# Splitting a second matrix ahead of a pair's first products, and a later gate after a pair, in a two-layer decoder trunk

## The chip, the cores and the metric

The kernel runs on one core of a Trainium2 chip. The metric is the device time of one execution in microseconds (us); the time of a kernel is the median of several runs. Lower is better.

## What is computed

Two decoder layers over 256 positions of width 1024, fp32 throughout. The even layer has sparse attentions and a dense SwiGLU; the odd layer has a dilated attention and an expert SwiGLU: every token goes to two of eight experts, each with three matrices, 1024 x 3584, 1024 x 3584 and 3584 x 1024.

```python
def swiglu(x, w1, w3, w2):
    return (jax.nn.silu(x @ w1) * (x @ w3)) @ w2
...
def moe_swiglu(x2d, router, w1, w3, w2):
    logits = (x2d @ router).astype(F32)
    top_val, top_exp = lax.top_k(logits, TOP_K)
    gates = jax.nn.softmax(top_val, axis=-1)
...
        return (jax.nn.silu(xb @ w1[e]) * (xb @ w3[e])) @ w2[e]
```

The change is about the expert SwiGLU. Every matrix of it is read once from memory.

## The kernel before

**Two ways to multiply.** TensorE (PE) is fast with operands of type fp32r, which keep less of a number than fp32. So a tile of a matrix is *split*: `split` (L226) calls `parts` (L221), where ScalarE (ACT) writes `hi`, the tile rounded to fp32r (L222), and VectorE (DVE) writes `lo`, the tile minus `hi` (L223). `mm3` (L231 to L234) then makes three fp32r products: `hi` with the activations' high part, `lo` with it (L233), `hi` with their low part (L234); the first of them is L232. The `hi` and `lo` tiles, 128 x 1024 each, come from a pool of five buffers (`WB`). The other way, `up2` (L285) and the first half of `down` (L651), multiplies the raw fp32 tile without a split, with the tokens of *two* experts side by side: each has 64 columns of PE and its own half of the output's partitions.

**Blocks.** Experts 0 to 3 hold up to 128 tokens and are worked on alone; experts 4 and 5, and 6 and 7, hold up to 64 each and are worked on as pairs. Each expert's 3584 columns are cut into seven chunks of 512 (the last pair's seventh into two of 256). One chunk of an expert, or of a pair, is a *block*. `swiglu` goes through a list `items` in which two alone blocks and one pair block follow each other; there are 28 alone blocks and 15 pair blocks, here counted from 0, and the last two are pairs. Block N below is the N-th pair block.

**What a block does**, in the order of the program (`swiglu`, the loop over `items`): the first matrix's products start (`up` or `up2`, a generator that is advanced by `step(u, 2)`); then `gate_T` transposes the gated activations of the *preceding* block (L625 if that is a pair, L632 if alone) and splits them into `gh` on ACT and `gl` on DVE (L634, L635); then the rest of the first products, and the silu on ACT into `sl` (L700); then `down` for the preceding block: it loads the second matrix, splits it and adds its products to the accumulators `acc`; then the third matrix's products, and the multiply of `sl` by them on DVE (L713), which the next block's gate transposes. For the first chunk of an expert (`pre`) the preceding block's `down` is worked off before the first products.

For an alone block, `down` reads and splits so:

```python
                for q in range(r, nr if last else r + 2, m):
                    v = load(w2, c0 // P + q, m, 0, D)
                    ws += [split(v[:, j:j + 1, :]) for j in range(m)]
```

A load (L218) is a DMA of 1 MB, issued on SyncE (SP) into a ring of slots named `raw`. Each engine works in order. The order in which the program is written is not the final one: a scheduler places each instruction by when its operands are ready, and keeps the program's order as the tie's. What stands on each engine in the end is a list that can be printed; the rows below come from it.

Of the kernel before, what the change touches and what calls it, by code (L numbers as in the profile page):

```python
# [17 lines left out]
P = 128  # L18
D = 1024
# [133 lines left out]
def trunk(ctx: ExitStack, tc: tile.TileContext, a, out, R=6, WB=5, NF=16):  # L153
# [17 lines left out]
    def nm(s):  # L171
        uid[0] += 1
        return f"{s}_{uid[0]}"
# [31 lines left out]
    def raw():  # L205
        slot = "raw"
        if late:
            slot = late.pop(0)
            if slot == "x":
                return xp.tile([P, 2 * D], F32, tag="x", name=nm("raw"), bufs=2)  # L210
            late.append(slot)
        return rawp.tile([P, 2048], F32, tag=slot, name=nm("raw"), bufs=R if slot == "raw" else 1)

    def load(w, r0, nr, c0, ncol):
        t = raw()
        v = t[:, :nr * ncol].rearrange("p (k f) -> p k f", k=nr)
        src = w.at(r0, nr, c0, ncol)
        nc.sync.dma_start(v if len(src.shape) == 3 else t[:, :nr * ncol], src)  # L218
        return v

    def parts(v, hi, lo, by):  # L221
        A.activation(hi, v, AF.Copy)  # L222
        by.tensor_sub(lo, v, hi.bitcast(F32))  # L223
        return hi, lo

    def split(v, by=V):  # L226
        _, k, n = v.shape
        t = [wp.tile([P, 1024], F32R, tag=q, name=nm(q)) for q in ("hi", "lo")]
        return parts(v, *(q[:, :k * n].rearrange("p (k f) -> p k f", k=k) for q in t), by)
# [34 lines left out]
    def up(outs, w, c0, ncol, sta, ws=None, between=None):  # L264


        if ws is None:
            for q in pieces(w, c0, ncol, 2):
                for o, s in zip(outs, sta):
                    products(o, s, *q)  # L270
                yield
        else:
            for i in range(len(sta)):
                for q in ws:
                    products(outs[i], sta[i], *q)
                if i == 0 and between:
                    between()

    def up2(o, ws, c0, ncol, sta):

        for r in (0, 4):
            vs = [load(w, r, 4, c0, ncol) for w in ws]
            for k in range(4):
                for i, v in enumerate(vs):
                    TE.matmul(o[i * 64:(i + 1) * 64, :ncol], lhsT=sta(r + k, i), rhs=v[:, k, :], start=r + k == 0,  # L285
                              stop=r + k == KT - 1)
                if k % 2:
                    yield
# [5 lines left out]
    def step(g, n=1):  # L294
        for _ in range(n):
            next(g, None)

    def end(g):
        for _ in g:
            pass  # L300
# [290 lines left out]
    w1, w3, w2 = W["even_w1"][0], W["even_w3"][0], W["even_w2"][0]  # L591
# [9 lines left out]
    ws = ahead(w1, *chunks[0])  # L601
# [14 lines left out]
    def swiglu(items, ws, between=None, behind=None, next_ws=None, tail=None, rare=None):  # L616

        def gate_T(it, g):  # L620
            n = it[4]
            if isinstance(it[0], tuple):
                pt, t = wk(), fa("gt")
                for j in range(n // P):
                    TE.transpose(pt[:, j * P:(j + 1) * P], g[0][:, j * P:(j + 1) * P], ident)  # L625
                A.copy(t[:, :n], pt[:, :n])  # L626
                return t
            gs = []
            for q in g:
                pt = wk()  # L630
                for j in range(n // P):
                    TE.transpose(pt[:, j * P:(j + 1) * P], q[:, j * P:(j + 1) * P], ident)  # L632
                gh, gl = fb("gh"), fb("gl")
                A.activation(gh[:, :n], pt[:, :n], AF.Copy)  # L634
                V.tensor_sub(gl[:, :n], pt[:, :n], gh[:, :n].bitcast(F32))  # L635
                gs.append((gh, gl))
            return gs

        def down(it, gs, fill=iter(())):
            w1, w3, w2, c0, n, sta, accs, first, last, pre, post = it  # L640
            nr = n // P
            accs = accs()
            if isinstance(w1, tuple):
                m = 1 if tail and it is items[-1] else 2
                for r in range(0, nr, m):
                    ws = [load(w, c0 // P + r, m, 0, D) for w in w2]
                    for j in range(m):
                        for d in range(2):
                            for i, w in enumerate(ws):
                                s = slice((r + j) * P + i * 64, (r + j) * P + (i + 1) * 64)  # L650
                                TE.matmul(accs[0][d][i * 64:(i + 1) * 64, :], lhsT=gs[:, s],  # L651
                                          rhs=w[:, j, d * 512:(d + 1) * 512], start=first and r + j == 0,
                                          stop=last and r + j == nr - 1)
                            step(fill)
                end(fill)
                if post:
                    post()
                return
            for r in range(0, nr, 2) if not last else [0]:
                ws = []  # L660
                m = 1 if tail and it is items[-1] else 2
                for q in range(r, nr if last else r + 2, m):
                    v = load(w2, c0 // P + q, m, 0, D)
                    ws += [split(v[:, j:j + 1, :]) for j in range(m)]
                for i, (gh, gl) in enumerate(gs):
                    for d in range(2):
                        for j, (wh, wl) in enumerate(ws):
                            s = slice((r + j) * P, (r + j + 1) * P)
                            c = slice(d * 512, (d + 1) * 512)
                            mm3(accs[i][d], gh[:, s], gl[:, s], wh[:, 0, c], wl[:, 0, c],  # L670
                                first and r + j == 0, last and r + j == nr - 1)
                            step(fill)
            end(fill)
            if post:
                post()

        prev = after = None
        for it in items:
            if it is items[-1] and next_ws:
                after = next_ws()  # L680
            w1, w3, w2, c0, n, sta, accs, first, last, pre, post = it
            fill = pre() if pre else None
            if fill:
                if prev:
                    step(fill, 3)
                    down(prev[0], gate_T(*prev), fill)
                    prev = None
                else:
                    end(fill)
            sta = sta()  # L690
            p1 = [wk() for _ in sta]
            two = isinstance(w1, tuple)
            u = up2(p1[0], w1, c0, n, sta[0]) if two else up(p1, w1, c0, n, sta, ws, between)
            step(u, 2)
            if prev:
                gs = gate_T(*prev)
            end(u)
            s = [fa("sl") for _ in sta]
            for q, p in zip(s, p1):
                A.activation(q[:, :n], p[:, :n], AF.Silu)  # L700
            held = tail and it is items[-1]
            if prev and not held:
                down(prev[0], gs)
            if rare and it is items[26]:
                rare()
            p3 = [wk() for _ in sta]
            with tc.issue_after(behind) if ws else nullcontext():
                end(up2(p3[0], w3, c0, n, sta[0]) if two else up(p3, w3, c0, n, sta))
            ws = None
            if held:  # L710
                down(prev[0], gs)
            for q, p in zip(s, p3):
                V.tensor_mul(q[:, :n], q[:, :n], p[:, :n])  # L713
            prev = (it, s)
        down(prev[0], gate_T(*prev), *([tail()] if tail else []))
        return after and after + next_ws(4)
# [3 lines left out]
    accs = [[acc(), acc()] for h in range(2)]  # L720
    odd_in = W["odd_w_in"][0]
    ws = swiglu([(w1, w3, w2, c0, n, lambda: sta, lambda: accs, i == 0, i == len(chunks) - 1, None, None)
            for i, (c0, n) in enumerate(chunks)], ws, rest, behind, lambda r=0: ahead(odd_in, 0, 512, r))
    x2, sta, rest, (behind, _) = finish_ln(accs, x1, g2, b2)
# [22 lines left out]
    w1, w3, w2 = (W[q] for q in ("odd_w1", "odd_w3", "odd_w2"))  # L747
    ws = ahead(w1[0], 0, 512)
# [81 lines left out]
    with tc.issue_after(behind):  # L830
# [13 lines left out]
        for h in range(2):  # L844
# [7 lines left out]
            gt, gs = [tmp[:, 16 * h + 8 * i:16 * h + 8 * i + 8] for i in (1, 2)]  # L852
            q = cp.tile([P, 8], F32, name=nm("slots"))
# [240 lines left out]
    items = []  # L1094
# [59 lines left out]
```

## Time and profile before

| | us |
|---|---|
| median of three runs | 1375.55 (1373.21 to 1376.93) |
| the profiled execution's own time | 1373.32 |
| its span, first to last instruction | 1371.6 |
| PE busy | 1300.7 (95% of the span) |
| DVE busy | 784.7 (57%) |
| ACT busy | 614.1 (45%) |
| mean granted clock of PE, as a share of 2.4 GHz | 0.983 |
| read from memory | 424 MB, 310 GB/s over the span |

The profile is one execution. A row of its timeline has the start, the duration, the engine, the line, the operation, `output<-inputs`, the shape, and in brackets how long the engine idled before and what ended that. Matmuls are pipelined: what one costs is the distance between the starts of two, not its duration. A raw fp32 row appears as two entries (x2).

### The profile page before, as it was taken

The page shows a single profiled execution, that of the slowest core. Times are in us where ns is not written, and L with a number is a line of the kernel's source. Part 1 is how long each engine was busy: PE and PEld are TensorE (multiplying, and loading weights), DVE is VectorE, ACT ScalarE, POOL GpSimd, SP SyncE. Part 2 cuts the span into 40 slices and gives each one's busy share as a digit, 9 for nine tenths or more (in the row PEclk, how much of TensorE's full clock was granted, in tenths as well). Part 3 has the DMA queues.
Part 4 walks back from the last instruction along what each step waited for, and adds up shares of the span by engine and source line. Part 5 has one row for each costly group of instructions (what it writes and reads, how often), then busy time and mean ns, then how long its engine had stood idle before and what let it go on. Part 6 is the DMA issues. An engine that isn't in the chain of part 4 may idle for free. (4 is left out here: it accounts for less than half of the span.)

```text
span 1371.6 us, 16690 instructions
## 1 busy us (share of the span) xinstructions
PE 1300.7 (95%) x6130; PEld 886.3 (65%) x6130; DVE 784.7 (57%) x1201; ACT 614.1 (45%) x859; POOL 53.7 (4%) x40
## 2 busy tenths in 40 slices
PE   9998999999999899999999999999979999999996
PEld 7776888887777775564746556466646475646562
DVE  6988445547777574453645455464625474644463
ACT  5564434443555364453444445254525353544441
POOL 0012000101022100000000000000000000000001
PEclk9999999999999699999999999999999999999998
DMA  9532456654445489999999999997999998999964
GB/s 371 193 110 98 161 184 222 224 194 158 154 148 184 168 308 399 422 419 422 408 376 422 419 421 404 384 359 288 423 366 384 416 412 346 420 420 421 401 230 168
DMA packets 69191, 426.23 MB, mean 311 GB/s; under 512 B 7920, under 2 KB 16368, under 8 KB 19824
## 3 DMA queue, kind: packets, MB, share of 16 engines
q1 hardware_dynamic: 68096, 421.70, 78.0%
q0 software_dynamic: 864, 3.15, 0.7%
q8 instruction: 50, 0.82, 0.2%
q14 instruction: 37, 0.30, 0.1%
q10 hardware_dynamic: 144, 0.26, 0.1%
HBM read 424.03 MB, written 1.05 MB: 310 GB/s over the span
## 5 line engine op out<-in xcount | busy, mean ns | idle before, releaser
L223 DVE TENSOR_TENSOR lo<-raw,hi 128x1024 fp32r<-128x1024 f32 (+1 forms) x454 | 535.0, 1219 | 236.6 <-ACT hi L222 235.7
L222 ACT ACTIVATE hi<-raw 128x1024 fp32r<-128x1024 f32 (+2 forms) x472 | 467.1, 1034 | 230.6 <-PE wk L234 124.1
L285 PE MATMUL wk<-raw,xg 128*64 128x512 f32 (+1 forms) x960 | 213.1, 575 | 5.5 <-PEq L890 5.3
L233 PE MATMUL wk<-lo,xg 128*128 128x512 f32 x448 | 177.8, 397 | 5.3 <-DVE lo L223 5.2
L232 PE MATMUL wk<-hi,xg 128*128 128x512 f32 x448 | 178.3, 398 | 0.5 <-DVE x L1057 0.5
L234 PE MATMUL wk<-hi,xg 128*128 128x512 f32 x448 | 175.2, 391 | 0.0
L713 DVE TENSOR_TENSOR sl<-sl,wk 128x512 f32<-128x512 f32 (+1 forms) x55 | 36.3, 666 | 227.3 <-PE wk L285 139.3
L285 PEld LDWEIGHTS wk<-raw,xg 128*64 128x64 f32 x960 | 69.2, 138 | 128.1 <-issue 121.6
L232 PE MATMUL acc<-hi,gh 128*128 128x512 f32 x312 | 118.5, 400 | 15.1 <-ACT hi L222 14.5
L233 PE MATMUL acc<-lo,gh 128*128 128x512 f32 x312 | 122.7, 395 | 4.7 <-DVE lo L223 4.7
L234 PE MATMUL acc<-hi,gl 128*128 128x512 f32 x312 | 121.6, 392 | 1.4 <-DVE gl L635 1.2
L232 PEld LDWEIGHTS wk<-hi,xg 128*128 128x128 f32 x448 | 84.4, 188 | 37.2 <-issue 19.5
L233 PEld LDWEIGHTS wk<-lo,xg 128*128 128x128 f32 x448 | 84.4, 188 | 26.3 <-DVE lo L223 8.9
L651 PE MATMUL acc<-raw,gt 128*64 128x512 f32 x448 | 100.9, 598 | 0.3 <-ACT gt L626 0.3
L234 PEld LDWEIGHTS wk<-hi,xg 128*128 128x128 f32 x448 | 84.4, 188 | 16.9
L700 ACT ACTIVATE sl<-wk 128x512 f32<-128x512 f32 (+1 forms) x55 | 32.0, 582 | 138.4 <-PE wk L285 74.3
L232 PEld LDWEIGHTS acc<-hi,gh 128*128 128x128 f32 x312 | 58.0, 188 | 36.5 <-ACT hi L222 22.0
L232 PE MATMUL wk<-hi,xT 128*128 128x512 f32 (+1 forms) x192 | 72.4, 377 | 0.3 <-ACT xT L315 0.3
L233 PEld LDWEIGHTS acc<-lo,gh 128*128 128x128 f32 x312 | 58.6, 188 | 21.7 <-DVE lo L223 9.4
L233 PE MATMUL wk<-lo,xT 128*128 128x512 f32 (+1 forms) x192 | 71.7, 373 | 0.0
L234 PE MATMUL wk<-hi,xT 128*128 128x512 f32 (+1 forms) x192 | 71.5, 373 | 0.0
L651 PEld LDWEIGHTS acc<-raw,gt 128*64 128x64 f32 x448 | 35.2, 137 | 54.7 <-issue 54.0
(208 smaller groups left out, 1359.3 us busy)
## 6 DMA issues: line engine op xcount, KB each, us to landing
raw<-in_odd_w SPq DMA_DIRECT2D x326, 1024.0 KB, 9.6
raw<-in_even_w SPq DMA_DIRECT2D x31, 1024.0 KB, 4.9
raw<-in_odd_w_in SPq DMA_DIRECT2D x12, 1024.0 KB, 4.8
raw<-in_odd_w SPq DMA_DIRECT2D x20, 512.0 KB, 5.4
raw<-in_even_w_in SPq DMA_DIRECT2D x8, 1024.0 KB, 11.7
raw<-in_even_w_out SPq DMA_DIRECT2D x4, 1024.0 KB, 5.4
raw<-in_odd_w_out SPq DMA_DIRECT2D x4, 1024.0 KB, 5.2
raw<-in_even_w SPq DMA_DIRECT2D x4, 512.0 KB, 3.6
```

What stands on the lines that cost most here:

```text
L222: A.activation(hi, v, AF.Copy)
L223: by.tensor_sub(lo, v, hi.bitcast(F32))
L232: TE.matmul(o, lhsT=sh, rhs=wh, start=first, stop=False)
L233: TE.matmul(o, lhsT=sh, rhs=wl, start=False, stop=False)
L234: TE.matmul(o, lhsT=sl, rhs=wh, start=False, stop=last)
L285: TE.matmul(o[i * 64:(i + 1) * 64, :ncol], lhsT=sta(r + k, i), rhs=v[:, k, :], start=r + k == 0, stop=r + k == KT - 1)
L651: TE.matmul(accs[0][d][i * 64:(i + 1) * 64, :], lhsT=gs[:, s], rhs=w[:, j, d * 512:(d + 1) * 512], start=first and r + j == 0, stop=last a ...
L700: A.activation(q[:, :n], p[:, :n], AF.Silu)
L713: V.tensor_mul(q[:, :n], q[:, :n], p[:, :n])
```

## The change

The loads and splits of the second matrix become a generator, `rows_of`. When a block is a pair and the preceding one is alone, all of it is run before the pair's first products are written down, and `down` takes the finished tiles. Blocks 0 and 7 have their `down` ahead anyway, and block 14 follows a pair; it acts on the other 12. The second part: after a pair, the next block's first products are advanced by three steps, not two, before the gate.

```diff
-        def down(it, gs, fill=iter(())):
+        def rows_of(it):
+
+            w2, c0, n, last = it[2], it[3], it[4], it[8]
+            nr = n // P
+            for r in range(0, nr, 2) if not last else [0]:
+                ws = []
+                for q in range(r, nr if last else r + 2, 2):
+                    v = load(w2, c0 // P + q, 2, 0, D)
+                    ws += [split(v[:, j:j + 1, :]) for j in range(2)]
+                yield r, ws
+
+        def down(it, gs, fill=iter(()), rows=None):
...
-            for r in range(0, nr, 2) if not last else [0]:
-                ws = []
-                m = 1 if tail and it is items[-1] else 2
-                for q in range(r, nr if last else r + 2, m):
-                    v = load(w2, c0 // P + q, m, 0, D)
-                    ws += [split(v[:, j:j + 1, :]) for j in range(m)]
+            for r, ws in rows or rows_of(it):
...
             two = isinstance(w1, tuple)
+
+            rows = list(rows_of(prev[0])) if two and prev and not isinstance(prev[0][0], tuple) else None
             u = up2(p1[0], w1, c0, n, sta[0]) if two else up(p1, w1, c0, n, sta, ws, between)
-            step(u, 2)
+            step(u, 3 if prev and isinstance(prev[0][0], tuple) else 2)
...
-                down(prev[0], gs)
+                down(prev[0], gs, rows=rows)
...
-                down(prev[0], gs)
+                down(prev[0], gs, rows=rows)
```

In the rows below a tile's name has its number behind it. In the changed kernel's list L708 and L721 are what L700 and L713 are before.

PE in block 11, before. `L285` are the pair's first products (output `wk_9281`), `L632` the gate's transposes, `acc` the second matrix's products; the left-out rows are more of the same two `raw` in turn, 16 rows of `L285` in all, and then 24 of `acc`:

```order
L234 MATMUL wk_9235<-hi_9270,xg_8752 128x512
L285 MATMUL wk_9281<-raw_9282,xg_7349 64x512
L632 MATMUL wk_9294<-cst,sl_9189 128x128 x4
L285 MATMUL wk_9281<-raw_9284,xg_7349 64x512
...
L285 MATMUL wk_9281<-raw_9303,xg_7390 64x512
L285 MATMUL wk_9281<-raw_9305,xg_7390 64x512
...
L232 MATMUL acc_8939<-hi_9319,gh_9299 128x512
L232 MATMUL acc_8940<-hi_9319,gh_9299 128x512
L233 MATMUL acc_8939<-lo_9320,gh_9299 128x512
L234 MATMUL acc_8939<-hi_9319,gl_9300 128x512
```

PE in the same place with the change; left out are rows of `raw` behind the first three, ten of `acc` less those shown, six more rows of `raw` and then 12 of `acc`:

```order
L285 MATMUL wk_9281<-raw_9302,xg_7349 64x512
L632 MATMUL wk_9314<-cst,sl_9189 128x128 x4
L285 MATMUL wk_9281<-raw_9304,xg_7349 64x512
...
L232 MATMUL acc_8959<-hi_9284,gh_9319 128x512
L233 MATMUL acc_8959<-lo_9285,gh_9319 128x512
L285 MATMUL wk_9281<-raw_9323,xg_7390 64x512
L234 MATMUL acc_8959<-hi_9284,gl_9320 128x512
...
L234 MATMUL acc_8960<-hi_9288,gl_9320 128x512
L285 MATMUL wk_9281<-raw_9325,xg_7390 64x512
...
L232 MATMUL acc_8959<-hi_9294,gh_9319 128x512
```

What was 1 row, gate, 15 rows, 24 products is now 1 row, gate, 7 rows, 2 products, 1 row, 10 products, 7 rows, 12 products. The number of instructions is the same.

PE in block 3, before, where the gate stands behind eight rows:

```order
L285 MATMUL wk_5677<-raw_5678,xg_4423 64x512
L285 MATMUL wk_5677<-raw_5680,xg_4423 64x512
...
L632 MATMUL wk_5690<-cst,sl_5629 128x128 x4
L285 MATMUL wk_5677<-raw_5699,xg_4464 64x512
L285 MATMUL wk_5677<-raw_5701,xg_4464 64x512
...
L232 MATMUL acc_5713<-hi_5717,gh_5695 128x512
```

and with the change:

```order
L285 MATMUL wk_5677<-raw_5698,xg_4423 64x512
L632 MATMUL wk_5710<-cst,sl_5629 128x128 x4
L285 MATMUL wk_5677<-raw_5700,xg_4423 64x512
...
L232 MATMUL acc_5733<-hi_5680,gh_5715 128x512
L233 MATMUL acc_5733<-lo_5681,gh_5715 128x512
L234 MATMUL acc_5733<-hi_5680,gl_5716 128x512
L285 MATMUL wk_5677<-raw_5719,xg_4464 64x512
L232 MATMUL acc_5733<-hi_5684,gh_5715 128x512
...
L232 MATMUL acc_5733<-hi_5690,gh_5715 128x512
L285 MATMUL wk_5677<-raw_5721,xg_4464 64x512
```

Eight rows, gate, eight rows, 24 products have become 1, gate, 7, 3 products, 1, 10, 7, 11; the same holds for block 10.

DVE around block 11, before: `sl_9189` is the multiply of the alone block, `sl_9315` that of the pair, the four `lo` between them belong to the alone block's second matrix:

```order
L223 TENSOR_TENSOR lo_9271<-raw_9258,hi_9270 128x1024
L713 TENSOR_TENSOR sl_9189<-sl_9189,wk_9235 128x512
L635 TENSOR_TENSOR gl_9300<-wk_9294,gh_9299 128x512
L223 TENSOR_TENSOR lo_9320<-raw_9317,hi_9319 128x1024
L223 TENSOR_TENSOR lo_9324<-raw_9317,hi_9323 128x1024
L223 TENSOR_TENSOR lo_9342<-raw_9339,hi_9341 128x1024
L223 TENSOR_TENSOR lo_9346<-raw_9339,hi_9345 128x1024
L713 TENSOR_TENSOR sl_9315<-sl_9315,wk_9361 128x512
```

and with the change:

```order
L223 TENSOR_TENSOR lo_9271<-raw_9258,hi_9270 128x1024
L223 TENSOR_TENSOR lo_9285<-raw_9282,hi_9284 128x1024
L721 TENSOR_TENSOR sl_9189<-sl_9189,wk_9235 128x512
L223 TENSOR_TENSOR lo_9289<-raw_9282,hi_9288 128x1024
L223 TENSOR_TENSOR lo_9295<-raw_9292,hi_9294 128x1024
L223 TENSOR_TENSOR lo_9299<-raw_9292,hi_9298 128x1024
L635 TENSOR_TENSOR gl_9320<-wk_9314,gh_9319 128x512
L721 TENSOR_TENSOR sl_9335<-sl_9335,wk_9361 128x512
```

One `lo` stands ahead of the alone block's multiply, three between it and `gl`. On ACT the four `hi` stand ahead of `gh` and the pair's silu, where they stood behind both. On SP the two loads of the second matrix stand ahead of the pair's four loads of its first matrices, where they stood behind them.

## Rows read from the trace of the kernel before

**Rows 1.** Waits of PE, 540 to 1345 us (us in total, times, longest)

```profile
PE acc L232 <- ACT hi L222: 14.5, 9, 1.6
PE acc L233 <- DVE lo L223: 4.7, 9, 0.5
PE wk L625 <- DVE sl L713: 3.9, 10, 0.5
```

**Rows 2.** Timeline of PE in block 11 (start, us, what ended the idle time)

```profile
1195.90 1.07 PE L285 MATMUL wk<-raw,xg 128*64 128x512 f32 x2
1196.90 0.66 PE L632 MATMUL wk<-cst,sl 128*128 128x128 f32 x4
1197.49 7.08 PE L285 MATMUL wk<-raw,xg 128*64 128x512 f32 x30
1206.20 0.73 PE L232 MATMUL acc<-hi,gh 128*128 128x512 f32 x2 [1.63 <-ACT hi L222]
1207.46 0.51 PE L233 MATMUL acc<-lo,gh 128*128 128x512 f32 x1 [0.53 <-DVE lo L223]
...
1212.71 0.65 PE L285 MATMUL wk<-raw,xg 128*64 128x512 f32 x2
```

**Rows 3.** Timeline of ACT around block 11

```profile
1185.58 5.79 ACT L222 ACTIVATE hi<-raw 128x1024 fp32r<-128x1024 f32 x6
1197.60 0.60 ACT L634 ACTIVATE gh<-wk 128x512 fp32r<-128x512 f32 x1 [6.23 <-PE wk L632]
1204.61 0.60 ACT L700 ACTIVATE sl<-wk 128x512 f32<-128x512 f32 x1 [6.41 <-PE wk L285]
1205.10 5.79 ACT L222 ACTIVATE hi<-raw 128x1024 fp32r<-128x1024 f32 x6
```

**Rows 4.** Timeline of DVE around block 11

```profile
1186.66 6.90 DVE L223 TENSOR_TENSOR lo<-raw,hi 128x1024 fp32r<-128x1024 f32 x6 [0.69 <-ACT hi L222]
1196.01 0.69 DVE L713 TENSOR_TENSOR sl<-sl,wk 128x512 f32<-128x512 f32 x1 [2.44 <-PE wk L234]
...
1206.18 4.63 DVE L223 TENSOR_TENSOR lo<-raw,hi 128x1024 fp32r<-128x1024 f32 x4 [7.26 <-ACT hi L222]
```

**Rows 5.** Timeline of PE in block 3, which has no such wait

```profile
683.74 0.39 PE L233 MATMUL wk<-lo,xg 128*128 128x512 f32 x1
683.97 0.39 PE L234 MATMUL wk<-hi,xg 128*128 128x512 f32 x1
684.29 3.65 PE L285 MATMUL wk<-raw,xg 128*64 128x512 f32 x16
687.87 0.66 PE L632 MATMUL wk<-cst,sl 128*128 128x128 f32 x4
688.46 3.65 PE L285 MATMUL wk<-raw,xg 128*64 128x512 f32 x16
692.04 0.50 PE L232 MATMUL acc<-hi,gh 128*128 128x512 f32 x1
692.38 0.39 PE L233 MATMUL acc<-lo,gh 128*128 128x512 f32 x1
...
697.79 0.65 PE L285 MATMUL wk<-raw,xg 128*64 128x512 f32 x2
```

**Rows 6.** Timeline of PE in block 13, whose rows have 256 columns

```profile
1321.17 1.95 PE L285 MATMUL wk<-raw,xg 128*64 128x256 f32 x16
1324.57 0.74 PE L232 MATMUL acc<-hi,gh 128*128 128x512 f32 x2 [1.45 <-ACT hi L222]
```

**Rows 7.** A steady cycle by windows (busy; clock, DMA share, GB/s); a load's issue; landings 1170 to 1182

```profile
1195.90:1256.99 61.09, 58.07 (x254) 35.21 (x254) 30.96 (x29) 26.66 (x30) 0.00 (x0) 1.00 1.01 421
...
1174.43 0.33 SPq L218 DMA_DIRECT2D raw<-in_odd_w  x1
...
DMA to landing us min/median/max: 8.4/11.8/15.6
```

## The prediction

> **What bounds the kernel now.** I read the profile's page first: TensorE (PE) is busy for 95% of the span, so time goes only where PE idles or does slow work. Then PE's waits from 540 to 1345 us, the expert phase [rows 1]. The reader is to see two lines with nine entries each: PE stands before the first product of a second matrix, `acc L232`, until ScalarE's `hi` is there (14.5 us in nine, so 1.61 each), and before `acc L233` until VectorE's `lo` is there (4.7 in nine, 0.52 each). These are nine of the 15 pair blocks. The third line (`wk L625`, 3.9 in ten) is the gate of the pair itself, which the change's second part aims at.
>
> Then the timelines of one such block [rows 2 to 4]. PE does one row of the pair's first product (1195.90), the gate transposes of the alone block before it (1196.90), the other 15 rows (1197.49), and then waits. ACT idles 6.23 us before `gh` and 6.41 before the pair's silu `sl` at 1204.61; only behind that silu does it start the second matrix's `hi` at 1205.10, although the data was there. DVE idles 7.26 for the same reason. So the stall is one of order, not of capacity: ACT and DVE have the time for four splits in the same block.
>
> **What the stall costs.** From the 15 rows' start to the pair's third product, 1197.49 to 1212.71, are 15.22 us [rows 2]. Block 3 has the same end without a stall: 8 rows and 24 products from 688.46 to 697.79, 9.33 us [rows 5]. A pair's two experts run side by side, so a row of one and a row of the other fill one slot: 30 entries take 7.08 us (eight slots, the last half filled), 16 entries 3.65 (four slots), so a slot is (7.08 - 3.65)/4 = 0.857. Block 11 has four slots more than block 3, 3.43. The stall therefore costs 15.22 - 9.33 - 3.43 = **2.46 us** a block.
>
> **What the change adds.** (a) No work is added on any engine: four `hi`, four `lo` and two loads are moved, 12 of 15 blocks (not the two where the second matrix comes first, nor the last, whose predecessor is a pair). (b) On PE the order shows that the products of the second matrix, now ready early, slide in among the rows of the pair: 1 row, gate, 7 rows, 2 products, 1 row, 10 products, 7 rows, 12 products, where it was 1, gate, 15, 24.
>
> A lone row costs a whole slot: from 1195.90 to the gate at 1196.90 one row takes 1.00, and eight rows from 684.29 to 687.87 take 3.58, that is 3.43 and 0.15, so that one row is 0.85 [rows 2, 5]. The slots were 1 + 8 = 9 and become 1 + 4 + 1 + 4 = 10: 0.857 more.
>
> Each change from 128-column products to rows of 64 columns and back costs too. Products follow each other at 0.23 (683.74 to 683.97). Into the rows it is 0.32 (684.29), 0.09 more; out of them the first product comes at 692.04, 0.15 after the slots end (688.46 + 3.43 = 691.89), and the second after 0.34, 0.11 more. Together **0.35** for there and back [rows 5]. The stretches of rows go from two to four, so two pairs more: 0.70. The Trainium skill, "TensorEngine Tiling (Array Packing)", Key Properties, speaks against this order: changing the tiling mode drains the engine. If each change were a full drain, a pair would cost the tails of the last product (0.39 - 0.23) and of the last row (3.65 - 3.43), 0.38, and the total below would fall from 3.7 to 3.1; the row's 0.35 is what I take.
>
> Sum of a steady block: 2.46 - 0.857 - 0.70 = **0.90 us gained**. Blocks 2, 4, 5, 8, 9, 11 and 12 are such: 6.3.
>
> Block 6 closes an expert. It has the same waits; there the order splits the combine's transposes, with one stretch of rows more and no slot more beyond the steady pattern: at worst another 0.35. I take 0.7, between 0.55 and 0.9.
>
> Block 13 has rows of 256 columns, so a slot is half, 0.43. Eight rows at 1321.17 would end at 1321.17 + 1.71 + 0.15 = 1323.03, and the product starts at 1324.57, 1.54 late [rows 6], with the second wait 2.3 in all. It goes from 9 to 10 slots and from three stretches to four: 2.3 - 0.43 - 0.35 = 1.5 gained.
>
> Blocks 3 and 10 have no stall to lose, and the order gives them the broken pattern too: 8, gate, 8 becomes 1, gate, 7, 3 products, 1, 10, 7, 11. Slots 8 to 10 and stretches two to four: 1.71 + 0.70 = 2.42 lost each, **4.84** together. Blocks 0, 1, 7 and 14 keep their order on PE.
>
> The second part (the gate one step later after a pair) moves the gate on PE only behind blocks 0 and 1; in the other transitions PE's order is the same row for row, so the third line of rows 1 stays. I cost it at nothing.
>
> **What hides the moved work.** ACT: `hi` for the alone block ends at 1185.58 + 5.79 = 1191.37 and `gh` starts at 1197.60 [rows 3]; four at 0.97 fit into the 6.23 between. They need buffers of the ring of five, freed as PE consumes the pieces of the third product, one per 6 products (6 x 0.23 = 1.37) up to 1195.9, when the pair's row starts: the last `hi` ends by my estimate at 1195.4. Without that cover `gh` and the silu would be late by what is over. DVE: the six `lo` end at 1186.66 + 6.90 = 1193.56; the first new `lo` (1.15) stands ahead of the alone block's multiply `sl` and ends at 1194.7, before the 1196.01 at which that multiply can start anyway [rows 4], 1.3 to spare. The other three stand between it and `gl`: 1196.70 + 3 x 1.15 = 1200.2, `gl` ends at 1200.9. PE wants `gl` only with the third product, 1197.49 + 3.43 + 0.15 + 0.57 + 0.95 = about 1202.6. SP and the DMA queue: the pair's four loads now stand behind two more of 1 MB. A steady cycle moves 24 of 1.0486 MB at 421 GB/s [rows 7], 2.49 each, so they come 5.0 later; the fourth was issued at 1174.43 and landings take at most 15.6, so 1190.0, and it is used from 1197.49 + 4 x 0.857 = 1200.9: covered. By the same rate a cycle of 61.09 can't fall below 24 x 2.49 = 59.8; 0.9 fits into that 1.3. What is late next in the steady cycle is the transition from the pair to the next alone block, untouched.
>
> **Total.** 6.3 + 0.7 + 1.5 - 4.84 = 3.7 us. The profiled execution took 1373.32 (span 1371.6), so it would take 1369.6; against the median of the runs, 1375.55, which is 2.2 above it, **1371.9**. That is 0.27%, and about 0.3% (4.1 us) is what a measurement of this kernel can tell from no change: same, by little. Bounds of the unknown price: an extra change pair may be free, or its way out (0.15 + 0.11) may be paid twice, since the row between is single: 0.61. There are 7 x 2 + 1 + 1 + 2 x 2 = 20 extra pairs, so 7.0 us to the one side, 5.0 to the other: 1364.9 to 1376.9.
>
> **Rivals.** First, *the changes cost nothing and only lone rows do*: 1364.9. For it: weights load beside running products. Against it: every change in rows 2 and 5 shows its gap. Second, *lone rows are free as well*, as when the next stretch's rows overlap: 8 x 2.46 + 2.3 = 22.0 gained, 1353.6; against it stands the 1.00 of the single row at 1195.90. Third, *slower: the new split holds up the multiply on DVE*. VectorE works in order. If the first `hi` gets its buffer only with the last piece of the third product (1195.8) and not before the first, `lo` ends at 1195.8 + 0.97 + 1.15 = 1197.9, the multiply at 1198.6, the gate comes 1.7 late instead of at 1196.90: each of eight blocks loses 1.7 - 0.9 = 0.8, and with +1.5 and -4.84 it is 9.7 slower, 1385.3. It decides from the point at which that `lo` ends after 1196.2. Against it: five buffers, four pieces. Fourth, *it doesn't do what it says*: the splits run early but the gain of the eight blocks goes into another wait (the transition, or a load behind the two moved ones); then +1.5 - 4.84 leave 1378.9, or with half the gain kept 1375.4.
>
> **How the numbers follow.** Forecast 0.66, of which 0.40 lie within 0.3% and 0.26 beyond it on the fast side, since 3.7 is near 4.1. First rival 0.15 and second 0.03, both faster. Third 0.08, slower. Fourth 0.08, 0.05 same and 0.03 slower. Faster 0.44, same 0.45, slower 0.11. The range is 1364.5 to 1377.0: it takes in both bounds and the first rival, and leaves out the second, the third and part of the fourth.
>
> **What would show it.** Right: both nine-entry lines gone from PE's waits, `hi` x10 in one stretch on ACT before `gh`, the pair's period 60.2 instead of 61.09, and in block 3 about 2.4 us more from 684.29 to the third product than the 13.50 there now. Wrong: a new wait at `L632` on `sl` (third rival), at `L285` on a load (fourth), block 3 unchanged in length (second), or single rows with no gap around them (first).

## The result: 14.3 us faster, and the profile after

The changed kernel takes 1361.42 us (median of four runs, 1360.79 to 1362.27), the kernel before 1375.72 beside it: 0.9899 of it, 95% interval 0.9882 to 0.9916. The forecast was 1371.9, with 1364.5 to 1377.0 as the range, and no change that can be told as the likeliest case (0.45, against 0.44 for faster). The time lies outside the range. The two profiled executions, 1373.32 and 1362.27, differ by 11.05; the other 3 us by which the medians differ more are looked for below.

First the waits of PE from 540 to 1345 us, the view of [rows 1], in the kernel after (us in total, times, longest):

```profile
PE wk L233 <- DVE lo L223: 5.4, 11, 0.6
PE wk L625 <- DVE sl L721: 5.1, 11, 0.6
PE acc L234 <- DVE gl L635: 0.9, 1, 0.9
PE wk L285 <- PEq L898: 0.8, 1, 0.8
```

Both lines with nine entries are gone. The fourth line here (`PEq` is PE's sequencer, the part that takes the instructions in order, and L898 a branch of the program) was in the same view before, and the prediction didn't take it up:

```profile
PE wk L285 <- PEq L890: 5.3, 1, 5.3
```

Block 11 on PE in the kernel after, which answers to [rows 2]:

```profile
1187.67 1.07 PE L285 MATMUL wk<-raw,xg 128*64 128x512 f32 x2
1188.67 0.66 PE L632 MATMUL wk<-cst,sl 128*128 128x128 f32 x4
1189.26 3.65 PE L285 MATMUL wk<-raw,xg 128*64 128x512 f32 x14
1192.84 0.50 PE L232 MATMUL acc<-hi,gh 128*128 128x512 f32 x1
1193.17 0.40 PE L233 MATMUL acc<-lo,gh 128*128 128x512 f32 x1
1193.49 1.07 PE L285 MATMUL wk<-raw,xg 128*64 128x512 f32 x2
1194.50 0.50 PE L234 MATMUL acc<-hi,gl 128*128 128x512 f32 x1
1194.83 0.39 PE L232 MATMUL acc<-hi,gh 128*128 128x512 f32 x1
...
1196.99 3.65 PE L285 MATMUL wk<-raw,xg 128*64 128x512 f32 x14
...
1203.52 2.79 PE L285 MATMUL wk<-raw,xg 128*64 128x512 f32 x12
```

From the first row to the third product are 15.85 us, where 1195.90 to 1212.71 were 16.81 before: no idle left, but a lone row at 1193.49 that takes 1.01 until the next product, and seven rows that take as long as eight. ACT and DVE after, which answer to [rows 3, 4]:

```profile
1186.41 1.06 ACT L222 ACTIVATE hi<-raw 128x1024 fp32r<-128x1024 f32 x1 [0.30 <-PE wk L234]
1189.36 0.60 ACT L634 ACTIVATE gh<-wk 128x512 fp32r<-128x512 f32 x1 [1.89 <-PE wk L632]
1200.68 0.60 ACT L708 ACTIVATE sl<-wk 128x512 f32<-128x512 f32 x1 [10.72 <-PE wk L285]
```

```profile
1187.77 0.69 DVE L721 TENSOR_TENSOR sl<-sl,wk 128x512 f32<-128x512 f32 x1 [1.28 <-PE wk L234]
1188.38 3.49 DVE L223 TENSOR_TENSOR lo<-raw,hi 128x1024 fp32r<-128x1024 f32 x3
1191.79 0.69 DVE L635 TENSOR_TENSOR gl<-wk,gh 128x512 fp32r<-128x512 f32 x1
```

The last `hi` waits 0.30 for its buffer and ends 1.89 before `gh`; the multiply has 1.28 of idle ahead of it (1.3 was forecast), and `gl` ends at 1192.48, before PE wants it at 1194.50. The steady cycle, which answers to [rows 7], in a window from gate to gate, and the same window before:

```profile
1188.67:1248.74 60.07, 59.14 (x254) 35.14 (x253) 30.79 (x30) 26.89 (x30) 0.00 (x0) 1.00 1.01 420
```

```profile
1196.90:1257.92 61.02, 58.00 (x253) 35.14 (x252) 30.95 (x29) 26.66 (x30) 0.00 (x0) 1.00 1.01 421
```

0.95 less a cycle. Taken over the whole phase, from the starts of the gates L632 behind each pair block in both traces:

| stretch | by the sum of the prediction | measured, us |
|---|---|---|
| start to block 2 | 0 | +0.70 |
| blocks 2, 4, 5, 9, 11, 12 | -0.90 each | -0.84, -0.84, -0.94, -0.87, -0.89, -0.93 |
| blocks 3, 10 | +2.42 each | +2.49, +2.45 |
| blocks 6 and 7, with the change of expert | -0.7 | -2.13 |
| **block 8** | **-0.90** | **-8.27** |
| blocks 13, 14 and the end | -1.5 | -0.97 |

They add up to -11.04. The +0.70 of the first line is chance: nearly all of it is there at 485 us, ahead of the experts, a point that the 14 traces reach between 483.97 and 486.30. Nearly all that was forecast is there; block 8 is worth nine times its forecast.

Block 8 is item 26 of the list, behind whose second matrix the program has the overflow branch (`rare`): code for tokens beyond an expert's room, skipped for this input. PE in that place before:

```profile
1017.03 0.39 PE L234 MATMUL acc<-hi,gl 128*128 128x512 f32 x1
1022.72 9.95 PE L285 MATMUL wk<-raw,xg 128*64 128x512 f32 x32 [5.30 <-PEq L890]
```

and after:

```profile
1014.50 0.39 PE L234 MATMUL acc<-hi,gl 128*128 128x512 f32 x1
1015.72 7.09 PE L285 MATMUL wk<-raw,xg 128*64 128x512 f32 x32 [0.83 <-PEq L898]
```

The wait is 4.47 shorter, and the same 16 rows take 2.86 less. The windows over these rows (the granted clock is the third number from the end), before and after:

```profile
1022.72:1032.60 9.88, 9.88 (x33) 3.12 (x33) 0.00 (x0) 0.00 (x0) 0.00 (x0) 0.71 0.81 289
```

```profile
1015.72:1022.74 7.02, 7.02 (x33) 2.62 (x33) 0.00 (x0) 0.00 (x0) 0.00 (x0) 1.00 0.98 379
```

Behind the idle time PE ran for a while at 1.2 GHz, half its clock: 0.71 is the mean over the 16 rows. 4.47 + 2.86 + 0.90 = 8.23, which is block 8. Why the wait shrank stands in what PE's sequencer did at the branch's line (the load of the number that the branch tests, then the jump; duration in ns, min/median/max, then the start in us), before:

```profile
L890 PEldq TENSOR_LOAD <-number x1: 488/488/488, 1015.5 to 1015.5; - x1
L890 PEldq COMPARE_BRANCH  x1: 6132/6132/6132, 1016.1 to 1016.1; - x1
```

and after:

```profile
L898 PEldq TENSOR_LOAD <-number x1: 484/484/484, 1009.2 to 1009.2; - x1
L898 PEldq COMPARE_BRANCH  x1: 5432/5432/5432, 1009.8 to 1009.8; - x1
```

The jump takes 5.4 to 6.1 us in both. Before, the sequencer came to the branch at 1015.53, 0.06 behind the end of the last `lo` of the block's four (1015.47), when PE had 1.9 us of products left; in the other three traces in which block 8 has its stall and the branch its old place (before_again, step_only, not_p8) it is the same 0.06. After, all splits are long done; the sequencer comes there at 1009.2, with 5.7 us of products left, and the jump lies beside them. The jumps of ACT and DVE over the same code take 0.05 and 0.07 us, so the long one is PE's alone.

The Trainium skill, "Runtime: NRT & Kernel Launch", section Instruction fetch mechanics, says that a taken branch whose target isn't loaded yet has to fetch it first. The traces agree. The DMA view has queues for instructions, and on `q8`, whose packets are 16 KB, one packet moves while PE's sequencer jumps, in the kernel before (1016.12 to 1022.25) as in all ten traces with a long jump (queue: packets, MB, share of 16 engines):

```profile
q1 hardware_dynamic: 313, 2.19, 86.8%
q8 instruction: 1, 0.02, 1.1%
q14 instruction: 1, 0.01, 0.3%
```

That this packet holds the jump's target is not shown.

### The profile page after: what moved, and what is told of

Same layout as the page of the kernel before. It is cut to its first block, busy times and chain, and to the rows that moved or that the text cites. A ratio compares the mean times of both kernels' runs of the same rounds, so it can differ in the third digit from the quotient of the medians.

```text
span 1360.5 us, 16711 instructions
## 1 busy us (share of the span) xinstructions
PE 1314.6 (97%) x6130; PEld 887.5 (65%) x6130; DVE 783.2 (58%) x1201; ACT 617.4 (45%) x859; POOL 53.8 (4%) x40
## 5 line engine op out<-in xcount | busy, mean ns | idle before, releaser
L285 PE MATMUL wk<-raw,xg 128*64 128x512 f32 (+1 forms) x960 | 226.3, 570 | 0.8 <-PEq L898 0.8
L721 DVE TENSOR_TENSOR sl<-sl,wk 128x512 f32<-128x512 f32 (+1 forms) x55 | 36.3, 667 | 286.4 <-PE wk L285 218.7
L285 PEld LDWEIGHTS wk<-raw,xg 128*64 128x64 f32 x960 | 70.3, 137 | 124.1 <-issue 117.2
L232 PE MATMUL acc<-hi,gh 128*128 128x512 f32 x312 | 123.0, 403 | 0.8 <-ACT gh L634 0.6
L708 ACT ACTIVATE sl<-wk 128x512 f32<-128x512 f32 (+1 forms) x55 | 32.0, 582 | 186.0 <-PE wk L285 124.2
L234 PEld LDWEIGHTS acc<-hi,gl 128*128 128x128 f32 x312 | 58.6, 188 | 20.9 <-issue 6.5
```

The lines of the kernel that those rows point to most:

```text
L232: TE.matmul(o, lhsT=sh, rhs=wh, start=first, stop=False)
L234: TE.matmul(o, lhsT=sl, rhs=wh, start=False, stop=last)
```

## Experiments

Two theories: "branch", that block 8's gain is the jump, now hidden; "blocks", that the branch's wait varies by chance and every block is worth more than was summed. The first four runs:

```diff
p8_only: the splits early in block 8 alone, the gate's step as before
-rows = list(rows_of(prev[0])) if two and prev and not isinstance(prev[0][0], tuple) else None
+rows = list(rows_of(prev[0])) if rare and it is items[26] else None
-step(u, 3 if prev and isinstance(prev[0][0], tuple) else 2)
+step(u, 2)
not_p8: in every block but that
-rows = list(rows_of(prev[0])) if two and prev and not isinstance(prev[0][0], tuple) else None
+rows = list(rows_of(prev[0])) if two and it is not items[26] and prev and not isinstance(prev[0][0], tuple) else None
before_nobr, after_nobr: no branch, in the kernel before and in the changed one
-        with tc.If(nc.values_load(most, min_val=0, max_val=1) > 0):
+        if False:
```

> The first part of the change in block 8 alone (the pair block in front of the overflow branch), the second part left out. Theory 'branch': in the kernel before, PE's sequencer stood at the products that wait for the last lo and so reached the jump over the overflow code only 1.5 us before PE ran out of work; with the splits early it gets there some 5 us sooner and the jump lies beside products. Then this one block is worth what the two profiles differ by there, 8.2 us (0.9 of a steady block, 4.5 of PE's wait at the branch, 2.9 of rows at half clock behind that wait): about 1367.5, between 1366.5 and 1369, PE's wait for PEq at the branch under 1.5 us, the clock 1.0 behind it. Rival 'blocks': the branch's wait differs by chance from run to run and each block is worth more than I summed; then one block is worth 0.9 to 1.2: about 1374.7, and the wait at the branch stays 5.3.

Measured: 1368.53, 0.9948 of before (0.9935 to 0.9961); beside these four, before had 1375.19. One block of twelve gives 6.7 us. Gate to gate (from the gate of one pair, L625, to that of the next) block 8 is 8.20 shorter in its trace, as forecast. The waits of its trace:

```profile
PE acc L232 <- ACT hi L222: 12.9, 8, 1.6
...
PE acc L233 <- DVE lo L223: 4.2, 8, 0.5
...
PE wk L285 <- PEq L898: 0.8, 1, 0.8
```

Eight of the nine stalls are there and cost what they did; the wait at the branch is 0.8. "Blocks" falls.

> The change as it is, but block 8 works as before. 'Branch': the wait of 5.3 us at the branch and the rows at half clock behind it are back; what is left is the sum of the other blocks, 2.8 us by the two profiles: about 1372.9, between 1369.5 (if the median of before lies above its profile for another reason that the change also mends) and 1373.5. 'Blocks': about 1362.3, only 0.9 slower than the changed kernel.

Measured: 1368.62, 0.9955 (0.9943 to 0.9967): 6.6 faster than before, and 0.9 below the range. The branch's wait is back, but at 3.48, not 5.3, and the rows behind it take 8.78. In this trace eight products of block 8 follow each other at 0.43, half clock, behind the stall, so PE came later to the branch that the sequencer was already resolving. So the sign holds and the size was off; p8_only and not_p8 together give 13.2 of the 14.

> The kernel before without the overflow branch (the code for tokens beyond an expert's room, which this input never enters, is left out; its buffers are still taken). 'Branch': PE's 5.3 us and the 2.9 of half clock go: about 1367.5, between 1366.5 and 1368.5, all the nine waits of 1.63 and 0.53 stay. 'Blocks': the branch is worth under 1 us: about 1375.

Measured: 1367.37, 0.9943 (0.9930 to 0.9956), with all nine stalls (14.5 and 4.7) as before. The branch alone costs the kernel before 7.8 us; in the trace block 8 is 8.28 shorter without it.

> The changed kernel without the overflow branch (the same code left out). 'Branch': only the 0.8 us that is still exposed goes: about 1360.6, so that with the branch gone from both kernels the change is worth 3 to 7 us and not 14. 'Blocks': the change is worth 14 us with or without the branch.

Measured: 1361.98, 0.9906 (0.9892 to 0.9921), within a microsecond of the changed kernel. With no branch in either, the change is worth 1367.37 - 1361.98 = 5.4 us, with it 14. "Branch" holds.

The next four take the other terms of the sum one by one:

```diff
not_3_10: blocks 3 and 10 (items 11 and 32) as before
+rows = ... and it not in (items[11], items[32]) else None
held: the second matrix's products wait for the pair's last row of first products
+                    mm[0] = TE.matmul(o[i * 64:(i + 1) * 64, :ncol], ...)
-                down(prev[0], gs, rows=rows)
+                with tc.issue_after(mm[0].ins) if rows else nullcontext():
+                    down(prev[0], gs, rows=rows)
held_gate: held, and the gate waits for the pair's eighth row
-                gs = gate_T(*prev)
+                with tc.issue_after(mm[0].ins) if rows else nullcontext():
+                    gs = gate_T(*prev)
step_only: the kernel before with the second part of the change
-            step(u, 2)
+            step(u, 3 if prev and isinstance(prev[0][0], tuple) else 2)
```

> The change without blocks 3 and 10, which keep their splits behind the silu and so the unbroken order 8 rows, gate, 8 rows, 24 products. If a lone row costs a whole slot and a change between products and rows 0.35 us, as I summed it, each of the two gives back 2.42: about 1356.5, between 1355 and 1357.5. If broken order costs nothing there: 1361.4. If the two get a stall in place of the broken order: above 1361.

Measured: 1356.54, 0.9873 (0.9858 to 0.9888); before had 1374.89 beside these four. That is the forecast to the tenth, and in the trace the two blocks are 2.42 and 2.47 shorter than with the change: broken order costs 2.4 us a block where there was no stall to remove.

> The change with the products of the second matrix held on PE behind all rows of the pair's first products (the splits stay early), so that a steady block is 1 row, gate, 15 rows, 24 products, without stall. By the sum of the prediction each of ten blocks gains one slot and two changes more than the change, 1.56, and block 13 half of that: 16.4 in all, about 1345, between 1343 and 1348, if the loads keep up. Rival: a cycle can't fall below the 59.8 us that its 24 loads take; then the cycles stop there, new waits of PE or ACT for a load appear, and it is 1350 to 1357.

Measured: 1347.86, 0.9799 (0.9786 to 0.9812). The order on PE is 1, gate, 15, 24 and the cycle 58.53 us, below the 59.8 of the rival:

```profile
1199.67:1258.20 58.53, 57.60 (x252) 35.18 (x253) 30.78 (x30) 27.00 (x30) 0.00 (x0) 1.00 1.01 421
```

PE waits for no load. ACT does, which the rival named as a sign: its waits from 540 to 1345 us, in the kernel before and in held:

```profile
ACT hi L222 <- DMA raw<-in_odd_w: 0.8, 1, 0.8
```

```profile
ACT hi L222 <- DMA raw<-in_odd_w: 10.0, 8, 4.6
```

They lie beside PE's products and cost nothing here. Gate to gate the steady blocks are 1.52 to 1.61 us shorter than with the change, where 1.56 was summed. Block 8 is 3.38 longer: the wait at the branch is 2.79, not 0.83, and the 16 rows behind it take 9.99, not 7.02, at a mean granted clock of 0.70. That is 4.9 more than was summed for it, while blocks 6, 7 and 13 gave some 2 more than summed; so the time lies above the forecast's middle.

> As held, and the gate held behind the pair's first eight rows: 8 rows, gate, 8 rows, 24 products in every such block, one slot less, 0.857, in ten and 0.43 in block 13: 9.0 us, about 1336 if the loads keep up. Rival, loads as the bound: at the time of held, or at most 3 us less, with waits for loads in the steady cycles at a period of 59.8.

Measured: 1337.63, 0.9728 (0.9715 to 0.9742), 10.2 less than held where 9.0 were forecast. The steady blocks are 0.83 to 0.89 shorter than in held, as forecast, block 8 1.93, since less of it runs at half clock. The steady cycle is 57.67, so the loads don't bound the time yet and the rival falls; but ACT's waits for them grow again:

```profile
PE wk L287 <- PEq L902: 3.0, 1, 3.0
...
ACT hi L222 <- DMA raw<-in_odd_w: 14.3, 9, 3.7
```

> The second part of the change alone: the gate a step later after a pair. On PE the order differs only behind blocks 0 and 1, where ten rows of products change places with a gate. I priced it at nothing: 1375.2 within 1.5 us, all nine waits of 1.63 and 0.53 as before. Rival: it hides the waits at the gate (3.9 us in ten): about 1371.

Measured: 1375.53, ratio 1.0004 (0.9995 to 1.0013): nothing, as priced.

Then the branch moved, with nothing else changed, in the kernel before and in held_gate:

```diff
-            if rare and it is items[26]:
-                rare()
             p3 = [wk() for _ in sta]
...
                 end(up2(p3[0], w3, c0, n, sta[0]) if two else up(p3, w3, c0, n, sta))
+            if rare and it is items[26]:
+                rare()
```

> The kernel before, with nothing but the overflow branch moved: it stands behind the third product of block 8 and not ahead of it. The jump itself takes PE's sequencer 5.4 to 6.2 us in every trace so far, and the sequencer reaches it 16 products ahead of PE (after: 4 rows and 12 products left when it started; held: 3.8 us of products), unless a product that waits for its operand holds it up, as the last lo did in the kernel before. Behind 16 rows of the third product 16 ahead are 6.9 us. Theory 'branch': the wait falls from 5.3 to under 0.8 and the rows at half clock are gone: about 1367, as without the branch (1367.4), with all nine waits at the splits still there. Rival: the cost is the jump's own fetch beside the loads, wherever it stands, and an early split only happened to shift it: about 1375.

Measured: 1368.02, 0.9950 (0.9936 to 0.9963); before had 1375.38. One moved statement gives 7.4 us, half of what the change gives (the trace is that of its slowest run, 1371.59). PE no longer waits at the branch, but mainly for another reason than I gave: the sequencer came only 4.5 us ahead of PE, not 6.9, and the jump itself was short here:

```profile
L890 PEldq TENSOR_LOAD <-number x1: 487/487/487, 1022.4 to 1022.4; - x1
L890 PEldq COMPARE_BRANCH  x1: 445/445/445, 1023.0 to 1023.0; - x1
```

No packet moves on `q8` during this jump (1023.02 to 1023.46); its last one started at 1020.2:

```profile
q1 hardware_dynamic: 19, 0.10, 52.5%
```

In held_gate_late below it is the same: the jump takes 0.35, and the last packet started 5.3 us before it. So the move made the jump itself short, likely because the fetch lay ahead of it, and these two runs don't test whether queued products hide a long one; p8_only and the changed kernel do.

DVE, which now comes late to its own jump, makes PE wait instead, and half clock follows (products at 0.43, not 0.23):

```profile
1028.30 0.47 PE L232 MATMUL wk<-hi,xg 128*128 128x512 f32 x1 [1.43 <-DVEq L890]
...
1030.70 0.63 PE L233 MATMUL wk<-lo,xg 128*128 128x512 f32 x1
1031.13 0.63 PE L234 MATMUL wk<-hi,xg 128*128 128x512 f32 x1
```

> held_gate with the branch moved in the same way. In held_gate PE still waited 3.0 us at the branch, because 16 products of 0.23 are only 3.8 us, and ran 3.4 us at half clock behind it, 1.7. 'Branch': both go, about 1333, between 1332 and 1334.5. Rival: 1337.6 as held_gate.

Measured: 1335.42, 0.9715 (0.9702 to 0.9728): the fastest version, 40 us below the kernel before and 26 below the change. It is 2.2 faster than held_gate, not the 4.6 that was expected; the wait of 3.0 became one of 1.57 for DVE's jump, and eight products at 0.43 follow it here too.

Last, a second trace of both, for the 3 us by which the medians differ more than the first two traces:

> The kernel before once more, for a second trace. In the six traces so far with stalls of 1.63 and 0.53, 10 of 45 such stalls are followed within 2.2 us by one stretch of 3.4 us at half clock, the first trace of before by none. Theory: these stretches, 1.6 us each, are why the median of before lies above its first trace; in a second trace some of the nine stalls have one (two by the share so far), and the branch's wait of about 5 us and its half clock are there again. Rival: the runs differ by something in the first 500 us; then there is none at the stalls and the time differs from the first trace's before the experts begin.

Measured: 1374.86, ratio to before 0.9992 (0.9982 to 1.0002). In the trace one of the nine stalls is followed by half clock, which makes block 2 longer by 1.38 than in the first trace, and it is there at the branch again (the wait, 5.0, stands against a load in this trace, but the sequencer's jump ended only 0.5 before PE went on). One more stretch, 1.58, follows PE's wait of 1.18 us for `gl` at the change of expert (943.61), which is no stall of the nine. The first 484 us are 0.75 shorter than in the first trace, so the runs do differ there as well, here to the other side. What such a stretch looks like, in p8_only's trace, in windows over the stall and behind it:

```profile
812.00:816.00 4.00, 1.94 (x6) 0.43 (x3) 1.18 (x2) 2.76 (x4) 0.00 (x0) 0.98 1.01 397
816.00:819.00 3.00, 2.90 (x7) 2.33 (x8) 3.00 (x4) 2.94 (x4) 0.00 (x0) 0.50 1.02 426
819.00:822.00 3.00, 3.00 (x14) 2.41 (x13) 0.45 (x1) 0.69 (x1) 0.00 (x0) 0.96 1.03 431
```

Seven products where the next 3 us hold fourteen. Over all seven traces with such stalls, 11 of 54 are followed by it: nine stalls have 1.8 of them, 1.6 us each (8 products at 0.43 in place of 0.23), 2.9 us a run. This is an estimate from a count.

> The changed kernel once more, for a second trace. Theory: no stretch at half clock between 480 and 1345 us, as no stall and no long wait is left there; about 1361.5 and within 1.5 us of the first trace.

Measured: 1362.85, 0.9904 (0.9887 to 0.9921). Its trace ends 0.3 us from the first one's, and the clock is full from 480 to 1345 us, as in the first.

## Why the prediction was wrong

**The step that failed** is "Blocks 2, 4, 5, 8, 9, 11 and 12 are such: 6.3". Block 8 isn't such a block: its second matrix is followed by the branch, and the view of [rows 1] had the branch's 5.3 us as a line of its own. The prediction took from that view the lines that the change addresses and priced a stall removed in block 8 at a stall's price. It didn't ask what the early splits release beside PE's products: PE's sequencer, which came to the branch only when the last `lo` was there, and with it the jump behind. In its place: 8.3 us in block 8, of which 4.5 are the jump, now hidden, and 2.9 the half clock that followed the idle time. The runs show it from three sides: block 8 alone gives 6.7, the branch taken out of the kernel before gives 7.8, the branch only moved gives 7.4 (there because the jump itself became short).

**A second miss, smaller.** The stall was priced at 2.46 us from one block at full clock. The total stood on one trace in which none of the nine had a stretch at half clock behind it, though the median lay 2.2 above that trace; I carried that difference over to the changed kernel as if it would stay. In the seven traces of kernels without these stalls the only such stretch in the expert phase away from the branch's wait is the one behind DVE's jump in held_gate_late, so the change removes them too. But the wait for `gl` at the change of expert stays with the change (0.94 us, where it was 1.18), and not_p8 has half clock behind it. That the stretches make most of the 3 us rests on the count and its price, not on a run that takes them away alone; 0.6 of the 3 is the start of the two traces.

**What held.** The price of a steady block (0.90, measured 0.84 to 0.94), of blocks 3 and 10 (2.42, measured 2.49 and 2.45, and 4.9 for both in not_3_10), of the second part (nothing, step_only), and the cover on ACT and DVE. A lone row and a change between products and rows cost what [rows 2, 5] gave, which held and held_gate confirm by taking them away. So the first two rivals fall. Every change shows its gap after, too: 1193.17 to 1193.49 into the row is 0.32 and 1194.50 to 1194.83 behind it 0.33, where products follow each other at 0.23. The Trainium skill, "TensorEngine Tiling (Array Packing)", Key Properties, says that changing the tiling mode drains the engine. The gaps fit that; that a drain makes them the trace doesn't show. The third rival didn't come: the gate waits for no multiply beyond 0.3 us. The bound on loads was wrong for a single cycle: cycles of 58.53 and 57.67 ran without PE waiting for a load, though 24 loads at 421 GB/s take 59.8. What shrinks is the loads' lead, as ACT's waits for them show (0.8 us before, 10.0 in held, 14.3 in held_gate); it lasted to the end of the phase. Blocks 6 and 7 gave 2.1 and not 0.7: PE's waits of 0.33 for `y` (881.24) and 0.55 for `x` (908.00) in the trace before are gone after, and what makes the rest is open.

**The range** failed with the sum: 3.7 of the gain was seen, the branch's 7.4 and the stretches' 2.9 make it 14.0, against 14.3 measured. That the two come so close is in part luck, since the last term is an estimate. (The slow bound takes 20 x 0.26 as 5.0; it is 5.2, which changes nothing here.)

## What to carry to other kernels

Read every line of the waits of the engine that bounds the kernel, not only those that a change is aimed at, and ask of each whether the work that is moved stands ahead of it. Here PE's sequencer came to the branch 0.06 us behind the operand that PE's products waited for, and its jump started that much later. Put a branch where each engine has products or splits queued that don't wait for anyone: with 5.7 us of products queued a jump of 5.4 us cost PE 0.8, with 1.9 us queued one of 6.1 cost 5.3. Work that becomes ready early also moves in front: see in the final order what it breaks up, and hold it back where that costs more than the stall; held and held_gate took 13.6 and 23.8 us from the changed kernel in this way.

## What the runs showed of the hardware that I had not expected

A jump over skipped code took PE's sequencer 5.4 to 6.2 us in ten traces and 0.35 to 0.45 in two (before_late, held_gate_late). In the ten a packet of 16 KB moved on the instruction queue `q8` during the jump, in the two it had moved 2.8 and 5.3 us before. That it is the packet with the target is likely and not shown; how to place a branch so that the packet comes first is open. Idle times of 1.6 and 0.5 us within a microsecond were followed in 11 of 54 cases by some 3 us at a granted clock of 1.2 GHz; so were one wait of 0.94 us (not_p8) and two of 1.18 (before_again, step_only). After the branch's 5 us the clock fell in both traces of the kernel before.
